# Six loads first, or stores and loads queued by turns: the order of one DMA queue in an RMSNorm kernel

## The chip, the cores and the metric

The kernel runs on one core of one Trainium2 chip. The metric is the device time in microseconds (us), lower is better; every time below is a median of several executions, and all runs of this study were of the fast state with a granted clock of 1.0. The core has compute engines (here ACT, the ScalarE, DVE, the VectorE, and POOL, the GpSimd) and a sequencer SP, which in this kernel only issues transfers and waits. The transfers run on 16 DMA engines, fed here by one queue, q1.

## The reference

```python
def reference(x, gamma, eps):          # x: 16 x 1024 x 512 float32, gamma: 512
    rms = np.sqrt(np.mean(x ** 2, axis=-1, keepdims=True) + eps)
    x_norm = x / rms * gamma
    return np.maximum(x_norm, 0).astype(np.float32)
```

Each of 16384 rows of 512 numbers is scaled by the inverse of its root mean square, multiplied by gamma and cut at zero. 33.5 MB have to come in and 33.5 MB have to go out.

## The kernel before

The rows are taken in eight chunks of 4 MB, 16 rows per partition (32 KB in each of 128 partitions). Six chunks fit into the on-chip memory at once (`nslots = 6`). A chunk is worked on in place: a load fills a slot, ACT squares and sums and takes the root, DVE multiplies and takes the maximum, a store empties the slot. Work goes in groups of eight rows per partition (`G = 8`), so a chunk is two groups (`per = 2`). I write L0 to L7 for the loads and S0 to S7 for the stores.

```python
    # SP: the order of the one queue
    for m, (i, a, r) in enumerate(loads):      # L0 comes in two halves
        if i < nslots:
            load(m)                            # L0 .. L5 at once
    nxt = nslots
    for i in range(nchunks):
        nc.sync.wait_ge(done, per * (i + 1))   # DVE has finished chunk i
        store(i)
        if i >= 1 and nxt < nchunks:
            nc.sync.wait_ge(sem_st[nxt - nslots], 16)   # the slot is free
            ...                                # L6 after S1, L7 after S2
            nxt += 1
    # ... POOL passes "chunk landed" on to ACT; ACT loop per group:
    #     8 x activation(Square, accum_out), 1 x activation(Sqrt)
    # DVE loop per group (16 groups)
    nc.vector.reciprocal(out=rstd[...], in_=rms[...])
    for j in range(G):
        nc.vector.scalar_tensor_tensor(out=row, in0=row, scalar=rstd[...],
                                       in1=gamma_sb, op0=ALU.mult, op1=ALU.mult)
    nc.vector.tensor_scalar_max(out=blk, in0=blk, scalar1=0.0).then_inc(done, 1)
```

## Time and profile before

| | before |
|---|---|
| time, median of 3 (later of 6) | 162.89 us (162.99) |
| span of the profiled run | 161.2 us |
| q1, share of 16 DMA engines | 97.4% |
| DVE busy | 126.0 us, 78% |
| ACT busy | 86.3 us, 54% |

This is the timeline of SP's queue in the kernel before: start in us, length in us from the first to the last of the merged issues, what was issued, how many.

```profile
0.94 3.59 SPq L74 DMA_DIRECT2D slots<-in_x_dram  x7
31.14 16.83 SPq L78 DMA_DIRECT2D out_dram<-slots  x2
72.07 0.34 SPq L74 DMA_DIRECT2D slots<-in_x_dram  x1
72.45 0.68 SPq L78 DMA_DIRECT2D out_dram<-slots  x1
81.97 0.34 SPq L74 DMA_DIRECT2D slots<-in_x_dram  x1
82.36 64.50 SPq L78 DMA_DIRECT2D out_dram<-slots  x5
```

Seven load issues (L0 in halves, L1 to L5) leave in the first five microseconds. S0 and S1 follow when DVE has finished their chunks, at 31 and 48. L6 has to wait until S0 has emptied its slot, at 72, and L7 until 82. All this time the queue has transfers in it, so SP's waits cost nothing.

### The profile page before, as it was taken

The numbers are of one execution on the slowest core, as the hardware profiler recorded it, in microseconds if no ns is written. First come the engines' busy times: TensorE is split into PE (matmuls) and PEld (weight loads), VectorE is DVE, ScalarE is ACT, GpSimd is POOL, SyncE is SP. The second block draws the span as 40 slices with busy tenths as digits, with TensorE's granted clock in tenths as the row PEclk, the third lists the DMA queues.
The fourth block names the chain that finished last, engine by engine and source line by source line (L and its number), as shares of the span: only waits on it lengthen the run. The fifth ranks groups of instructions, "written<-read, shape, count | busy, mean of one in ns | idle before, by whom it ended". The sixth has DMA issues, their size and how long they took to land. (4 is left out here: it accounts for less than half of the span.)

```text
span 161.2 us, 1006 instructions
## 1 busy us (share of the span) xinstructions
DVE 126.0 (78%) x164; ACT 86.3 (54%) x273; POOL 0.2 (0%) x4
## 2 busy tenths in 40 slices
DVE  1103989898989898999999999999999999993000
ACT  3088929889988988988900298503994000000000
POOL 0000000000000000000000000000000000000000
DMA  5999999999999999999999999999999999999993
GB/s 155 433 439 431 496 390 415 496 390 399 512 390 390 512 399 390 390 399 512 390 399 504 399 399 496 407 399 488 407 407 488 407 407 480 415 407 464 431 390 138
DMA packets 2456, 67.12 MB, mean 416 GB/s; under 512 B 276, under 2 KB 276, under 8 KB 280
## 3 DMA queue, kind: packets, MB, share of 16 engines
q1 hardware_dynamic: 2448, 67.11, 97.4%
q10 hardware_dynamic: 8, 0.01, 0.0%
HBM read 33.56 MB, written 33.55 MB: 416 GB/s over the span
## 5 line engine op out<-in xcount | busy, mean ns | idle before, releaser
L115 ACT ACTIVATE junk<-slots 128x512 f32 x128 | 74.5, 582 | 30.8 <-ACTq L111 30.5
L139 DVE SCALAR_TENSOR_TENSOR slots<-slots,rstd,gamma_sb 128x512 f32 x128 | 86.2, 747 | 4.8 <-DVEq L136 4.8
L146 DVE TENSOR_SCALAR slots<-slots x16 | 36.7, 2294 | 2.4 <-DVEq L145 0.2
L115 ACT ACTIVATION_READ_ACCUMULATOR junk<-slots x128 | 23.9, 187 | 0.0
L133 DVE RECIPROCAL rstd<-rms x16 | 3.2, 197 | 6.4 <-DVEq L129 6.4
L122 ACT ACTIVATE rms<-ss,eps_sb x16 | 4.8, 301 | 3.0 <-ACTq L121 3.0
L126 DVE LOAD_MASK_SELECT gamma_sb<-gseed x1 | 0.0, 14 | 5.8 <-DMA gseed<-in_gamma_dram 5.8
L107 ACT ACT_TABLE_LOAD x1 | 1.3, 1283 | 2.8 <-issue 2.8
L100 DVE MEMSET gseed<- 128x512 f32 x1 | 0.5, 485 | 1.1 <-SPq L81 1.1
L126 DVE STREAM_SHUFFLE gamma_sb<-gseed 128x512 f32<-128x512 f32 x1 | 0.7, 716 | 0.0
L168 POOL MEMSET const-bfloat16-1.0<- 128x1 bf16 x1 | 0.1, 102 | 0.0
L168 POOL MEMSET const-uint8-127<- 128x1 uint8 x1 | 0.1, 102 | 0.0
L168 POOL MEMSET const-float32-1.0<- 128x1 f32 x1 | 0.1, 99 | 0.0
L168 POOL MEMSET const-float32-0.0<- 128x1 f32 x1 | 0.1, 98 | 0.2 <-issue 0.2
L101 DVE MEMSET eps_sb<- 128x1 f32 x1 | 0.1, 59 | 0.0
## 6 DMA issues: line engine op xcount, KB each, us to landing
out_dram<-slots SPq DMA_DIRECT2D x8, 4096.0 KB, 31.4
slots<-in_x_dram SPq DMA_DIRECT2D x7, 4096.0 KB, 30.4
slots<-in_x_dram SPq DMA_DIRECT2D x2, 2048.0 KB, 9.7
gseed<-in_gamma_dram ACTq DMA_DIRECT2D x1, 8.0 KB
```

Of the source, the lines that this page charges most:

```text
L100: nc.vector.memset(gseed, 0.0).then_inc(sem_z, 1)
L101: nc.vector.memset(eps_sb, eps).then_inc(sem_e, 1)
L107: nc.scalar.preload_act_table(ACTF.Sqrt)
L115: a = nc.scalar.activation(out=junk[:, j, :], in_=slots[:, bass.ds(base + j * d, d)], func=ACTF.Square, accum_out=ss[:, bass.ds(col + j, 1)])
L122: nc.scalar.activation(out=rms[:, bass.ds(col, G)], in_=ss[:, bass.ds(col, G)], func=ACTF.Sqrt, bias=eps_sb, scale=inv_d).then_inc(sq, 1)
L126: nc.vector.stream_shuffle(gamma_sb, gseed, [0] * 32)
L133: nc.vector.reciprocal(out=rstd[:, bass.ds(col, G)], in_=rms[:, bass.ds(col, G)]).then_inc(sv, 1)
L139: r = nc.vector.scalar_tensor_tensor(out=row, in0=row, scalar=rstd[:, bass.ds(col + j, 1)], in1=gamma_sb, op0=ALU.mult, op1=ALU.mult)
L146: nc.vector.tensor_scalar_max(out=blk, in0=blk, scalar1=0.0).then_inc(done, 1)
L168: nc = _bacc.Bacc("TRN2", target_bir_lowering=False, num_devices=1)
```

## The change

The intent is to let stores start earlier and to spread loads and stores evenly, by queueing each load from L4 on right behind a store: L4 behind S0, L5 behind S1, L6 behind S2, L7 behind S3. No engine's work changes.

```diff
--- before.py
+++ after.py
@@ -79,19 +79,19 @@
 
     ctx.enter_context(tc.manual_schedule(engines={mybir.EngineType.SP}))
     with tc.tile_critical():
+        ahead = 4
+        nst = 0
         for m, (i, a, r) in enumerate(loads):
-            if i < nslots:
-                load(m)
-        nxt = nslots
-        for i in range(nchunks):
+            if i > nst + ahead - 1:
+                nc.sync.wait_ge(done, per * (nst + 1))
+                store(nst)
+                nst += 1
+            if i >= nslots:
+                nc.sync.wait_ge(sem_st[i - nslots], 16)
+            load(m)
+        for i in range(nst, nchunks):
             nc.sync.wait_ge(done, per * (i + 1))
             store(i)
-            if i >= 1 and nxt < nchunks:
-                nc.sync.wait_ge(sem_st[nxt - nslots], 16)
-                for m, (c, a, r) in enumerate(loads):
-                    if c == nxt:
-                        load(m)
-                nxt += 1
 
         for m, (i, a, r) in enumerate(loads):
             nc.gpsimd.wait_ge(sem_ld[m], 16)
```

## The prediction

> **What bounds the kernel now.** I began with the page's busy shares by slice and its DMA queue part, because a kernel that moves 33.5 MB in and 33.5 MB out may well be a copy with some arithmetic beside it.
>
> ```profile
> DVE  1103989898989898999999999999999999993000
> ACT  3088929889988988988900298503994000000000
> DMA  5999999999999999999999999999999999999993
> DMA packets 2456, 67.12 MB, mean 416 GB/s; under 512 B 276, under 2 KB 276, under 8 KB 280
> q1 hardware_dynamic: 2448, 67.11, 97.4%
> ```
>
> The DMA row has no digit under 9 between the first and the last slice, and the one queue q1 fills 97.4% of the 16 engines' time. The transfer engines have no hole that a new order could close. The second view is the table of stretches, for the rate by what is in the queue (the columns are length, busy time of DVE, ACT and POOL, PE clock, DMA share, GB/s):
>
> ```profile
> 4.00:58.00 54.00, 41.65 (x56) 42.53 (x137) 0.00 (x0) 1.00 1.01 436
> 62.00:80.00 18.00, 17.11 (x21) 16.58 (x54) 0.00 (x0) 1.00 1.00 430
> 80.00:112.00 32.00, 30.21 (x41) 11.86 (x38) 0.00 (x0) 1.00 1.00 431
> 112.00:157.00 45.00, 32.70 (x41) 10.14 (x34) 0.00 (x0) 1.00 1.00 430
> ```
>
> In order these are loads alone, the stores S0 and S1, load and store by turns (L6, S2, L7, S3), and stores alone. All run at 430 to 436 GB/s. So I take one chunk of 4,194,304 bytes at 430 GB/s as D = 9.75 us, whichever way it goes. Sixteen of them are 156.0 us. The one-microsecond stretches show the queue near its rate from about 2.4 us (180 GB/s from 2 to 3, 360 from 3 to 4), so the data should end at 2.4 + 156.0 = 158.4. The trace has it nearly stopped at 158:
>
> ```profile
> 157.00:158.00 1.00, 0.00 (x0) 0.00 (x0) 0.00 (x0) 1.00 1.21 524
> 158.00:159.00 1.00, 0.00 (x0) 0.00 (x0) 0.00 (x0) 1.00 0.08 33
> ```
>
> The remaining 161.2 - 158.4 = 2.8 us are the last receipt and the program's end. The page's chain that ended last covers only 1% of the span, in DVE's last instruction; it doesn't follow the queue, so I don't use it. The timeline gives the second limit, DVE:
>
> ```profile
> 14.53 0.20 DVE L133 RECIPROCAL rstd<-rms  x1 [6.41 <-DVEq L129]
> 22.78 0.20 DVE L133 RECIPROCAL rstd<-rms  x1
> 31.02 0.20 DVE L133 RECIPROCAL rstd<-rms  x1
> 144.20 2.29 DVE L146 TENSOR_SCALAR slots<-slots  x1
> ```
>
> DVE starts its 16 groups of eight rows at 14.53, one each 8.245 us without a hole, and ends at 146.49 (14.53 + 16 x 8.245 = 146.45). Chunk i (two groups) is therefore finished, and its store may be issued, at about 31.0 + 16.49 i. The last store can go at 146.5, and 9.75 us of data from there alone end near 157. The DMA's 158.4 is barely 2 us later: **two limits lie side by side**, and neither has slack worth 2% (3.3 us).
>
> **What the Trainium skill says.** "DMA: Bandwidth & Descriptors", section "Where 436 GB/s comes from", puts the ceiling of the DMA ports at 435.2 GB/s; the 430 to 436 of the stretches agree, so the queue runs at its ceiling already. The same page, "Queues, rings and completion order", says that descriptors of one ring are consumed in order; the trace agrees, for S0 was issued at 31.1 and landed only near 72, 40.9 us later, behind the loads that were queued before it. "HBM Reference", section "Access", gives about 425 GB/s for a core that streams alone, which fits too. I found no page that gives a cost for a change of direction between loads and stores; for that I have only this trace.
>
> **The change part by part.** It removes no instruction that moves data, and the compute code, the six slots and the transfers are the same. What moves is the queue's order: L0 L1 L2 L3 S0 L4 S1 L5 S2 L6 S3 L7 S4 S5 S6 S7 in place of L0 to L5 S0 S1 L6 S2 L7 S3 to S7. The wait for chunk 0's result now stands ahead of L4, that for chunk 1 ahead of L5, and so on. The issue itself costs 0.34 us of the queue's engine (in its timeline: the load at 72.07), under the transfers in flight. Two things have to hold for the total to stay.
>
> First, the queue must not run dry while SP waits for DVE. With D = 9.75 the plan is (data start to end; when the store ahead can be issued, from DVE's clock plus 0.34 us):
>
> - L0 to L3: 2.4 to 41.4.
> - S0 issued 31.4, L4 directly behind: 41.4 to 51.2 and 51.2 to 60.9. In hand 10.0 us.
> - S1 issued 47.9, with L5: 60.9 to 80.4. In hand 13.0.
> - S2 issued 64.4, with L6: 80.4 to 99.9. In hand 16.0.
> - S3 issued 80.9, with L7: 99.9 to 119.4. In hand 19.0.
> - S4 issued 97.3: to 129.2, in hand 22.1. S5 113.8: to 138.9, in hand 15.4. S6 130.3: to 148.7, in hand 8.6. S7 146.8: 148.7 to 158.4, in hand 1.9.
>
> It never runs dry, so the data end at the same 158.4. The waits for a free slot fall away as waits: S0 lands near 52 and S1 near 72, when L6 and L7 are issued at 64 and 81. Before they held SP for 32.9 us in total (the waits of SP), which cost nothing there either, as the DMA row shows.
>
> Second, DVE must not starve, for now the loads land later. ACT starts a chunk about 1.7 us after my time for the end of its data (L6 90.2 by the same sum, ACT at 91.85; L7 109.7, ACT at 111.51), and needs 5.8 us for a group before DVE can start. So a chunk is ready for DVE 7.5 us after its data end, and DVE comes to it at 14.5 + 16.49 i:
>
> - chunk 4: ready 60.9 + 7.5 = 68.4, wanted 80.5, slack 12.1.
> - chunk 5: 87.9, wanted 97.0, slack 9.1.
> - chunk 6: 107.4, wanted 113.4, slack 6.0.
> - chunk 7: 126.9, wanted 129.9, slack 3.0.
>
> L4 and L5 land 9.75 and 19.5 us later than before, L6 and L7 9.7 us each, and all are still in time. The sum of the change is **0 us on the path**: removed 0, added 0, moved 0.
>
> **The rivals.**
> (a) Four more changes of direction (nine against five) cost time. Against it: 80 to 112, where the direction changes four times, ran at 431. If each cost 0.25 us unseen, four would add 1.0 us, giving 163.9.
> (b) The last chunk comes late: L7 is 19.5 us after S3 is issued, with 3.0 us of slack. If the mixed stretch ran 3% below 430, its 78 us (41.4 to 119.4) would take 2.3 us more, which uses up most of that slack and also moves the DMA's end by 2.3 us: 165.2. Nothing in the profile shows such a loss.
> (c) Mixing speeds the transfers, by reads and writes passing at the same time. The 4 or so GB/s between stretches are within the counting of whole packets, and the ceiling is reached already. Even then S7 can't leave before 146.8; taking its 1.9 us away gives 161.0, so 2% can't be won unless DVE gets quicker.
> (d) A smaller initial burst: five load issues at the start, not seven, could let the first half chunk land sooner, by perhaps 0.2 us of the 8.78 at which ACT starts. That would move DVE's end by as much, not the DMA's.
>
> **Range and chances.** The prediction is the time before, less nothing: 162.8 us, with 162.89 before. The range takes (c) at half its size below and (a) above, with some of (b): 161.8 to 164.4. Faster by over 2% means below 159.6, which DVE's end at 146.5 and the last store's 13.5 us from issue to landing (in its row by line) nearly forbid: 0.01. Slower by over 2% means above 166.1 and needs (a) four times as large or (b) doubled: 0.04. Within 2%: 0.95.
>
> **What would show it.** Right: the DMA row still all nines, about 97% for q1, DVE's groups still 8.245 us apart with its end near 146.5, S7 issued then and landing about 13.5 us later; L6 issued near 64 and L7 near 81 without a wait for a store; ACT's idle time before chunks 4 to 7 moved, its sum the same. Wrong: a DMA digit under 9 between slices 10 and 30 (queue dry), an idle entry for DVE before a RECIPROCAL after the first (starved), or a rate clearly off 430 GB/s between 41 and 119 us (direction).

## The result, and the profile after

| | before | after |
|---|---|---|
| time, median of 6 | 162.99 us (162.83 to 163.12) | 163.31 us (162.85 to 163.56) |
| ratio, 95% interval | | 1.0017 (1.0002 to 1.0033) |
| span of the profiled run | 161.2 us | 161.8 us |
| DVE's last instruction ends | 146.49 us | 146.34 us |

A ratio here is always the mean time of one kernel's fast runs over the mean time of the kernel before in the same rounds, so it is not quite the ratio of the medians that I quote. The time is the same within 2%, 0.5 us above the forecast of 162.8 and inside the range. The page after, slices and queue:

```profile
DVE  1103989898989898989899999999999999991000
ACT  3088829989988914892068910789008880000000
DMA  5999999989999899999999999999999999999990
DMA packets 2456, 67.12 MB, mean 415 GB/s; under 512 B 276, under 2 KB 276, under 8 KB 280
q1 hardware_dynamic: 2448, 67.11, 97.2%
```

The DMA row is full again but for two digits of 8, and q1 has the same packets, the same bytes and nearly the same share. By the prediction's own sign the second 8, in the slice from 52.6 us on, would mean a dry queue. It doesn't: by the trace's packet records (start, length and size of each packet; `prof` doesn't print them) the engines are idle for less than 0.05 us in any 4 us between 4 and 156. The row counts a packet of 1.2 us at its start, so a slice can come out short, and a second profile of the kernel before has such an 8 too. The ACT row is the one that moved: its pauses now lie before each chunk from the fifth on. The table of stretches after (length, busy DVE, ACT, POOL, PE clock, DMA share, GB/s):

```profile
4.00:40.00 36.00, 24.69 (x34) 26.35 (x86) 0.00 (x0) 1.00 1.01 434
44.00:80.00 36.00, 34.06 (x43) 23.10 (x75) 0.00 (x0) 1.00 0.99 427
80.00:118.00 38.00, 35.92 (x49) 21.25 (x68) 0.00 (x0) 1.00 1.01 437
120.00:157.00 37.00, 25.00 (x31) 10.63 (x34) 0.00 (x0) 1.00 1.01 435
```

Loads alone, then two stretches of stores and loads by turns, then stores alone: 427 to 437 GB/s, as before. A whole packet of 32 KB counts at its start in this view and 16 are in flight, so 0.5 MB may fall on either side of an edge; over 36 us that is 15 GB/s, and the differences mean nothing. SP's timeline after:

```profile
0.94 2.61 SPq L74 DMA_DIRECT2D slots<-in_x_dram  x5
30.99 0.34 SPq L78 DMA_DIRECT2D out_dram<-slots  x1
31.37 0.43 SPq L74 DMA_DIRECT2D slots<-in_x_dram  x1
...
63.95 0.34 SPq L78 DMA_DIRECT2D out_dram<-slots  x1
64.34 0.81 SPq L74 DMA_DIRECT2D slots<-in_x_dram  x1
80.44 0.34 SPq L78 DMA_DIRECT2D out_dram<-slots  x1
80.83 0.84 SPq L74 DMA_DIRECT2D slots<-in_x_dram  x1
```

L6 leaves at 64.3 and L7 at 80.8, right behind S2 and S3, as planned, and without a wait for a store. Last, the engines: DVE's groups, and the first instruction of ACT on chunks 6 and 7, from the timeline after.

```profile
14.38 0.20 DVE L133 RECIPROCAL rstd<-rms  x1 [6.80 <-DVEq L129]
22.63 0.20 DVE L133 RECIPROCAL rstd<-rms  x1
30.88 0.20 DVE L133 RECIPROCAL rstd<-rms  x1
144.05 2.29 DVE L146 TENSOR_SCALAR slots<-slots  x1
101.95 0.60 ACT L115 ACTIVATE junk<-slots 128x512 f32 x1 [8.31 <-ACTq L111]
121.91 0.60 ACT L115 ACTIVATE junk<-slots 128x512 f32 x1 [8.68 <-ACTq L111]
```

DVE still takes a group each 8.24 us and ends at 146.34. ACT starts chunk 7 at 121.91, some 10 us later than before, and is still ahead: DVE comes to that chunk at 129.78.

### The profile page after: what moved, and what is told of

Read it like the earlier page. It is cut to its first block, busy times and chain, and to the rows that moved or that the text cites. A ratio compares the mean times of both kernels' runs of the same rounds, so it can differ in the third digit from the quotient of the medians.

```text
span 161.8 us, 1006 instructions
## 1 busy us (share of the span) xinstructions
DVE 126.0 (78%) x164; ACT 86.3 (53%) x273; POOL 0.2 (0%) x4
## 3 DMA queue, kind: packets, MB, share of 16 engines
q1 hardware_dynamic: 2448, 67.11, 97.2%
## 5 line engine op out<-in xcount | busy, mean ns | idle before, releaser
L115 ACT ACTIVATE junk<-slots 128x512 f32 x128 | 74.4, 581 | 41.2 <-ACTq L111 41.2
```

Source lines behind the costliest of these rows:

```text
L115: a = nc.scalar.activation(out=junk[:, j, :], in_=slots[:, bass.ds(base + j * d, d)], func=ACTF.Square, accum_out=ss[:, bass.ds(col + j, 1)])
```

## The experiments

Theory A is the prediction's: one queue at its ceiling rate sets the end, its order is free as long as it never runs dry and DVE never starves. What each run tells apart:

**The small excess, and changes of direction.** The changed kernel was run again, and two versions of it in which the first four stores and L4 to L7 go in quarters of 1 MB, once in blocks (nine changes of direction, as in the changed kernel) and once alternating (33 changes). In both of these SP waits for the free slot of L6 and L7 ahead of the store before it, not behind it; the queue stayed full.

```diff
 for m, (i, a, r) in enumerate(loads):
     if i > nst + ahead - 1:
         nc.sync.wait_ge(done, per * (nst + 1))
-        store(nst)
+        for q in range(4):
+            store_q(nst, q)      # quarter_turns: store_q and load_q in one loop
+        for q in range(4):
+            load_q(m, q)
         nst += 1
 # the waits on these transfers count to 16 * 4
```

> The changed kernel once more, to see whether the small excess over the kernel before (ratio 1.0017) is there again. Theory A (the queue is full at its ceiling rate in both, the order costs nothing): ratio 0.999 to 1.001. Rival B (each of the four added changes of direction costs about 0.08 us): ratio 1.001 to 1.003.

> The changed kernel with the first four stores and L4 to L7 cut into quarters of 1 MB, in the same order (four quarters of S0, four of L4, and so on). It is the control for the next run: nine changes of direction as in the changed kernel. Theory A: within 0.5 us of the changed kernel, near 163.2. If smaller rows (8 KB for 32 KB per partition) cost something, it shows here and not in the comparison.

> The same quarters, alternating (a quarter of S0, a quarter of L4, ...): 33 changes of direction against 9 in the control. Theory A (a change of direction costs nothing): within 0.4 us of the control. Rival B (0.08 us for each, from 0.3 us for four): 24 x 0.08 = 1.9 us over the control. Rival C (mixing speeds the transfers): under the control, by at most the 2 us or so that the last store had in hand.

| run | median us | ratio to before, 95% interval |
|---|---|---|
| after_again | 163.41 | 1.0032 (1.0018 to 1.0046) |
| quarter_blocks | 164.81 | 1.0119 (1.0103 to 1.0136) |
| quarter_turns | 164.27 | 1.0092 (1.0076 to 1.0109) |

The excess is real: 0.3% this time, again clear of 1 and outside what theory A allowed. But it is not a price per change of direction: 24 more changes made the time 0.5 us shorter, where rival B wanted 1.9 us more. Rival B falls. The gain of 0.5 us is a little over what theory A allowed (0.4), and I come back to it. Cutting into quarters itself cost 1.4 us against the changed kernel (164.81 less 163.41), where theory A allowed 0.5: a miss. The page's q1 lines of quarter_blocks and quarter_turns lead to the cause:

```profile
q1 hardware_dynamic: 5904, 67.11, 97.6%
...
q1 hardware_dynamic: 5904, 67.11, 97.8%
```

The share of 16 engines' time is that of full use in all of them; 97.6% of a span of 163.0 us is 159.1 us of packets on each engine, against 97.2% of 161.8 = 157.3 in the changed kernel. By the trace's packet records a 32 KB row takes 1213 ns (the median) and four of 8 KB take 4 x 309 = 1236. There are 4096 of the short ones, 256 on each engine in place of 64 long ones: 64 x 23 ns = 1.5 us; the rest of the 1.8 is about what the completion records of 24 more transfers take, 24 x 9 ns. Packets on one engine overlap a little, so not all of this is lost: the eight chunks in quarters take 9.84 us each by their completion records, against 9.70 whole, 1.1 us in all. The alternating version has packets of the same median length, 309 ns; by the means (309.3 against 310.1 ns) it gains 0.2 us on each engine. Rival C had the sign of the 0.5 us right, but faster packets are at most that 0.2 of it.

**DVE faster, DVE slower.** If the queue alone sets the end, a faster DVE gains nothing; and a slower one costs what exceeds the reserve of the last store.

```diff
-nc.vector.tensor_scalar_max(out=blk, in0=blk, scalar1=0.0).then_inc(done, 1)
+nc.vector.tensor_scalar_max(out=blk[:, 0:d], in0=blk[:, 0:d], scalar1=0.0).then_inc(done, 1)   # fast_dve
+nc.vector.memset(pad, 0.0)        # slow_dve: put ahead of the unchanged maximum
```

> The changed kernel with the last maximum of each group done on 512 of its 4096 columns (wrong on purpose: negative values stay in the rest). DVE's group falls from 8.24 to about 6.3 us, so every store can be issued earlier. Theory A (the queue sets the end, the last store had about 1.9 us in hand): no gain, 162.8 to 163.3, and the queue ends at about the same 158.4 us of the span. Rival D (DVE's end and the last store's way set the end): 1 to 2 us faster.

> The changed kernel with one more memset of 128x512 in each of DVE's 16 groups (0.49 us by the memset in the profile, so 7.8 us or a little more in all; the result stays right). Theory A: the last store has 1.9 us in hand, so the time rises by what DVE's end rises less 1.9: about 6 us, to 169 (168 to 170.5). If DVE's end set the time already (nothing in hand): 171. If the queue alone counted: 163.

> The kernel before with the same added memset as in the changed kernel's slow version (there DVE ended 7.55 us later and the time rose by 4.65, so 2.9 us were in hand). If both orders lean on the same two limits, it takes the same 168.0 us (167.5 to 168.4), the 0.5 us between the orders gone, since the last store then leaves on an empty queue. If the changed order had lost some of its reserve to the later loads, this one would be faster by that.

The fast version (wrong result) took 163.21 us, ratio 1.0038 (1.0011 to 1.0065), against 1.0032 for the changed kernel in the same rounds: no gain. Its page and DVE's last instruction:

```profile
DVE  1103987789898898988920989129890398700000
DMA  5999999999999999999999999999999999999992
140.04 0.43 DVE L146 TENSOR_SCALAR slots<-slots  x1
```

DVE now has holes and ends at 140.47, 5.9 us earlier, and the DMA row is as full as ever. The earlier store only stood in the queue. Rival D falls.

The slow version took 167.96 us. DVE's last instruction ends at 153.90, 7.56 us later than in the changed kernel (146.34), and the time rose by 167.96 - 163.31 = 4.65 us, so 2.9 us were in hand, not 1.9 (to some 0.2, for the two medians are of different rounds). I had expected 169 (168 to 170.5) and missed just below. The table of stretches shows the new hole, on an empty queue:

```profile
152.00:153.00 1.00, 1.00 (x1) 0.00 (x0) 0.00 (x0) 1.00 0.00 0
153.00:154.00 1.00, 0.90 (x1) 0.00 (x0) 0.00 (x0) 1.00 0.00 0
154.00:155.00 1.00, 0.00 (x0) 0.00 (x0) 0.00 (x0) 1.00 1.22 524
```

The first packet of S7 starts at 154.76, 0.83 us after its issue at 153.93, and the last packet of S6 had ended at 150.06: a hole of 4.7 us, the rise in time to 0.1 us. The kernel before with the same added work took 167.92 us, as forecast: once the last store leaves on an empty queue, both orders take the same time, and the excess of the changed one is gone.

**How far ahead the loads must be.** The changed kernel's loop has the number of chunks loaded ahead of the first store as one constant.

```diff
-ahead = 4
+ahead = 3      # also 2, 5 and 6
```

> The changed kernel with three chunks ahead of the stores in place of four (L0 L1 L2 S0 L3 S1 L4 ...). By the sums of the prediction, S0 is issued at 31.4 with the queue full to 31.7, so just not dry; chunk 4 is ready 2.3 us before DVE wants it, chunk 5 0.7 us late, chunk 6 another 3.1, chunk 7 another 3.0; DVE ends 6.8 us later, the last store leaves at 153.5 on a queue that ran out at 148.7, and the time is 167.8 us. Theory A in this form: 166.5 to 169. If a store's order had no such price (the queue alone counts): 163.

> Two chunks ahead (L0 L1 S0 L2 S1 L3 ...). By the same sums the queue is dry from 21.9 to 31.4 us, each later chunk waits for the store before it and DVE starves at nearly every chunk: the data end near 192 and the time is 196.6 us (190 to 201).

> Five chunks ahead (L0 to L4, S0 L5 S1 L6 S2 L7 S3 ...). No wait is reached late: L6 waits for S0, landed near 62, and is issued behind S1's wait for DVE at 47.6, so SP holds until 62 with the queue full to 80.4. Theory A: 162.7 to 163.5, as both kernels.

> Six chunks ahead by the changed kernel's loop (L0 to L5, S0, then L6 once S0 has landed, S1, then L7 once S1 has landed, S2 ...): the kernel before without the second store that it queues behind the first. Theory A says that the queue runs dry twice, from the end of S0's data (70.7) to its receipt (72.0) and on to the first bytes of L6 (about 1.5 us later), and again behind S1: 2 x 2.9 us = 5.8 us, so about 168.7 us (166.5 to 170). If the receipt and the start are hidden by other packets: 163.

| chunks ahead | expected us | median us | ratio to before |
|---|---|---|---|
| 2 | 196.6 | 200.03 | 1.2274 |
| 3 | 167.8 | 169.27 | 1.0392 |
| 4 (the change) | 162.8 | 163.31 and 163.41 | 1.0017 and 1.0032 |
| 5 | 162.7 to 163.5 | 163.30 | 1.0024 |
| 6 | 168.7 | 169.49 | 1.0402 |

The sums found the cliff on either side and the floor between, and were 0.8 to 3.4 us short where something waits; the run with three ahead came out 0.3 us above its expected range, the others inside. ahead5 has an excess of 0.24%, but its interval (0.9997 to 1.005) takes in 1, so it proves nothing. With three ahead, DVE starves at three chunks, as forecast:

```profile
88.69 0.20 DVE L133 RECIPROCAL rstd<-rms  x1
99.22 0.20 DVE L133 RECIPROCAL rstd<-rms  x1 [2.20 <-DVEq L129]
...
118.89 0.20 DVE L133 RECIPROCAL rstd<-rms  x1 [3.10 <-DVEq L129]
...
138.48 0.20 DVE L133 RECIPROCAL rstd<-rms  x1 [3.01 <-DVEq L129]
```

The number in brackets is DVE's idle time before the instruction. Chunks 6 and 7 came 3.1 and 3.0 us late, exactly the sums. Chunk 5 came 2.2 us late, not 0.7; these 1.5 us are what the time exceeds the forecast by (169.27 less 167.8). The packet records of this run show 1.9 us of over-long packets between 40 and 52 us, which the sums don't have. With six ahead the queue runs dry, although DVE is far ahead:

```profile
70.00:71.00 1.00, 0.90 (x1) 1.00 (x5) 0.00 (x0) 1.00 1.14 492
71.00:72.00 1.00, 1.00 (x1) 1.00 (x4) 0.00 (x0) 1.00 0.01 0
72.00:73.00 1.00, 0.70 (x3) 1.00 (x5) 0.00 (x0) 1.00 0.00 0
73.00:74.00 1.00, 1.00 (x2) 1.00 (x4) 0.00 (x0) 1.00 1.94 524
```

S0's last packet ends at 71.83, SP issues L6 at 72.19, and L6's first packet starts at 73.16. The same happens behind S1 (94.71 to 96.04). The forecast counted 2.9 us for each stop, all of it as an empty queue. Its total came near, but in part by luck: the queue is empty for 1.3 us only, and on the mean engine, which had ended earlier, for 1.8. As much again goes to longer packets, which the forecast didn't have: 0.6 to 0.7 us when L6 or L7 starts, and 1.1 us late in that load, ahead of the next store. By the completion records L6 and L7 end 13.34 and 13.21 us after the store ahead of them, where a whole chunk takes 9.68. This is the wait that the kernel before hides by queueing S1 first, and that the change hides by issuing L6 so late that S0 has long landed.

**Where the 0.3 to 0.6 us come from.** The packet records let one see when each of the 16 DMA engines is done with a transfer: each ends its part with a 4-byte record. The kernel before was run once more for a second profile, and an order with still fewer changes of direction (three) was tried.

```diff
 for i in range(nchunks):
     nc.sync.wait_ge(done, per * (i + 1))
     store(i)
-    if i >= 1 and nxt < nchunks:
-        nc.sync.wait_ge(sem_st[nxt - nslots], 16)
-        ...                       # load chunk nxt
+    if i == 2:                    # few_turns: L6 and L7 both behind S2
+        for c in range(nslots, nchunks):
+            nc.sync.wait_ge(sem_st[c - nslots], 16)
+            load(c + 1)
```

> The kernel before itself, for a second profile and for the noise of the ratio: 0.999 to 1.001. In its first profile the completion writes of the last store run from 158.35 us on the earliest DMA engine to 159.56 on the latest; in the changed kernel's two profiles the latest are 160.19 and 160.30. Theory E (more mixing lets one engine fall further behind, which is the small excess): the latest again near 159.6, under 159.9. Rival F (the lag is chance from run to run): it may lie anywhere from 159.5 to 160.3.

> The order with the fewest changes of direction that six slots allow without running dry: L0 to L5, S0 S1 S2, L6 L7, S3 to S7 (three changes, against five before and nine changed). The queue is full to 90.6 when L6 is issued behind S2 at about 72, and L7 behind S1's landing at 82. Theory A: the same as the kernel before, ratio 0.999 to 1.001. Theory E: a little faster, 0.998 to 1.000, with the latest engine under 159.6. No version can be over 0.5% faster by its order alone if the packets take what they take now.

before_again took 162.85 us (ratio 1.0004, 0.9991 to 1.0018) and few_turns 162.72 us (ratio 0.9998, 0.9984 to 1.0012): no order that I tried beats the kernel before. This table is worked out from the packet records. "Last load before S0" is the mean over the engines of the time from the end of the load ahead to the end of that load; all other whole chunks outside the mixed part take 9.68 to 9.71 us. The end of S7 is given for the earliest engine, the mean and the latest, in us of the span.

| run | last load before S0 | S7 ends: earliest, mean, latest | latest behind earliest (lag) |
|---|---|---|---|
| before | 10.42 | 158.35, 158.71, 159.56 | 1.21 |
| before_again | 10.38 | 158.33, 158.73, 159.62 | 1.30 |
| few_turns | 10.42 | 158.25, 158.66, 159.29 | 1.04 |
| after | 10.62 | 158.44, 158.90, 160.19 | 1.75 |
| after_again | 10.62 | 158.83, 159.33, 160.30 | 1.47 |
| ahead5 | 10.68 | 158.61, 159.15, 160.08 | 1.47 |
| fast_dve (the order of after) | 10.65 | 158.44, 158.96, 159.84 | 1.40 |
| quarter_blocks | 10.69 | 159.64, 160.12, 161.45 | 1.81 |
| quarter_turns | 10.71 | 159.57, 159.97, 160.79 | 1.22 |

Two things add up. First, ahead of the first change from loads to stores some packets of the last load take longer, once, by 0.7 to 0.8 us in the order before and by 0.8 to 1.0 in the changed one. Later changes on a queue that stays full cost next to nothing: in after every later chunk takes 9.68 to 9.70 us in the mean, but for L7 with 9.77. After_again lost something there again, with 10.18 for L7, and slow_dve with 9.92 for L5. Where the queue runs dry or nearly so it isn't once: in ahead6 it came again behind each stop (the 1.1 us above), and in ahead3, where the queue stood idle for 0.14 us before S0, the chunks S0 and L3 took 10.63 and 10.85 us. Second, the end is set by the latest of 16 engines, and in the changed order the latest was further behind. For the profiled pair: the latest engine ends 160.19 - 159.56 = 0.63 us later, of which 0.19 us are in the mean and the rest is lag. In after_again it is the other way round: of 160.30 - 159.56 = 0.74 us, 0.62 are in the mean. The lag grows between 80 and 120 us (from 0.48 to 0.94 in before, 0.59 to 1.50 in after, 0.60 to 0.75 in few_turns), and by 0.25 to 0.29 more in the stores alone that follow, in all three alike.

My theory E, that more mixing makes more lag, fits these three, but not the quarters: quarter_turns mixes most and lags less than quarter_blocks (1.22 against 1.81), and that 0.6 us is most of what made it the faster of the pair. Nor is rival F, that the lag is chance from run to run, excluded: in fast_dve, with the order of after, it is 1.40 us, and at the end of S6, where the slow pair can be compared too, it is 1.20, 1.29 and 0.96 in the order before (slow_dve_before the last) and 1.74, 1.46, 1.40 and 1.10 in the changed one (slow_dve the last). What does keep apart in these profiles is the mean end of S6, 148.92 to 149.05 us against 149.22 to 149.65, and, narrowly, the last load before S0, 10.36 to 10.46 us (ahead6 included) against 10.52 to 10.71 (ahead5 and the quarters included). So what makes an engine fall behind stays open, and so does why the first change costs more in one order than in the other. Each profile is one run, and 0.3 us is the size at stake.

## Why the prediction was right

- **The bound.** Right. The queue is full in both, and the changed order moves the same bytes at the same rate. fast_dve shows it: DVE ended 5.9 us earlier and the time didn't move. By the completion records a whole chunk takes 9.68 us, loads and stores alike; 4,194,304 bytes in that time are 433 GB/s, just under the ceiling that the prediction cites. No run moved data faster; that the ports are what limits it is the word of "DMA: Bandwidth & Descriptors" and not shown here. (The 425 GB/s that the prediction takes from "HBM Reference" stands there in the section "Specifications (TRN2)"; the trace is 2% above it.) One reading was off without effect on the time: the stretches count a packet at its start, so the data end at 159.6 by the packet records, not at 158.4, and what follows is 1.6 us, not 2.8. The sum is the same.
- **The queue in hand.** Right in its order. Its smallest term, 1.9 us in hand at S7, was mis-sized: slow_dve measured 2.9 in the changed order, and the kernel before in the same way 7.43 - (167.92 - 162.76) = 2.3, where DVE's end went from 146.49 to 153.92. The step that fell short is the end of the data, as said above: in slow_dve the last packet of S6 ended at 150.06, not at 148.7, which gives 1.36 us more; and the first packet of S7 follows DVE's end by 0.86 us (153.90 to 154.76), so without the added work it could start at 146.34 + 0.86 = 147.20, 0.4 us later than the planned 146.8. 1.9 + 1.36 - 0.4 is the 2.9 measured.
- **DVE's slack.** Right within 1 us: ACT started chunk 6 at 101.95 and chunk 7 at 121.91, so with 5.8 us for a group DVE could have gone on at 107.8 and 127.7, and came at 113.29 and 129.78. That leaves 5.5 and 2.1 us where the sums had 6.0 and 3.0. The run with three chunks ahead shows what happens when this slack is used up.
- **ACT's idle time.** Wrong in a side point: its pauses moved, but their sum didn't stay, it rose from 30.8 to 41.2 us on the squaring line, because the last chunk now comes some 10 us later and ACT's work ends later. ACT isn't the bound, so it cost nothing.
- **Rival (a), four more changes of direction.** Its guess of 1.0 us was too large and its mechanism is refuted by the quarters: on a queue that stays full not each change costs, only the first one.
- **Rival (b), L7 too late through a slower mixed stretch.** Didn't happen; DVE never waited. (The "19.5 us after S3 is issued" is misread from the plan: 19.5 us run from the start of S3's data, 99.9, to the end of L7's, 119.4; from S3's issue at 80.9 they are 38.5. The slack of 3.0 doesn't depend on it.)
- **Rival (c), mixing speeds the transfers.** Didn't happen to any size that counts; at most 0.2 us in quarter_turns.
- **Rival (d), a smaller first burst.** DVE's first group began at 14.38 against 14.53, 0.15 us earlier, and gave nothing, as said. Other runs with the first seven issues began at up to 14.61, so this may be chance.
- **The sum of 0.** Off by the excess: 0.3 us by the medians of the first rounds and 0.7 by those of the second (163.41 against 162.75). What the prediction had at zero is longer packets ahead of the first change, some 0.2 us more of them in the changed order, and, from run to run, a slow chunk or an engine that lags; a plan with one D for all chunks and engines can't see them. Why they arise isn't shown.

## What to carry to other kernels

When one transfer queue is full from end to end at its ceiling rate, its order is worth nothing by itself: ask only whether the new order lets the queue run dry or an engine starve, by a table of "issued at, data from, data to, wanted at" for each transfer. Here such a table placed both cliffs (three chunks ahead starves DVE, six with a wait for each store empties the queue) within 1.5 us, and the flat floor between them; only the run with two ahead, far down the slope, was off by 3.4. Don't put a wait for a transfer's landing directly behind that transfer on the only queue (here each such stop cost over 3 us): keep another transfer queued behind it first, or issue it so late that it has landed.

## What the Trainium skill lacked or had wrong

- "DMA: Bandwidth & Descriptors" has no word on a change between loads and stores in one queue. Here the first one cost 0.7 to 1.0 us, and on a queue that stays full 24 further ones (33 against 9) cost nothing that shows (164.27 against 164.81 us); behind a stop of the queue 1.1 us came again (ahead6).
- The same page, section "Measured (HBM→SBUF, 128 partitions, SWDGE, issued from GpSimd)", has 78% of the peak for a transfer of 1 MB. The table is of transfers issued from GpSimd, and doesn't say what was queued around them. Issued from SP and queued behind others, 1 MB transfers cost only 1.4% in rate (9.84 against 9.70 us for 4 MB).
- The same page, section "Latency and other measured facts", gives about 600 ns to the first byte on this path. On an empty queue, from the start of the issue to the first packet's start, the trace has 0.83 us for a store (153.93 to 154.76) and 0.97 us for a load (72.19 to 73.16). The page doesn't say from where it counts; from the end of the issue, 0.33 us later, they are 0.50 and 0.64 us, near the page's 600 ns.
- No page says how far the 16 DMA engines drift apart over a long queue from SP. The same page and section say that engines 7 and 15 are usually slower, and call the guessed cause specific to transfers from GpSimd; the records here don't name the engine. On a queue that stayed full the earliest and the latest ended the last store 1.0 to 1.8 us apart, which is more than the 0.7 us by which the whole-chunk orders that keep the queue full differ (162.72 to 163.41).
